# A recurrent mixer whose chunk steps are set further apart, with state sums of both tiles in one PSUM bank and outputs in the other

## The chip, the cores and the metric

The kernel runs on one core of one Trainium2 chip. The metric is the device time of one launch in microseconds (us). The program holds two whole transformer-like blocks; the change touches one part of the second, the recurrent mixer.

## The reference

The input is x of 256 tokens by 2048 channels. The first block is a state-space mixer beside a latent attention, followed by a convolutional feed-forward. The second block normalizes, projects once (`w_in`), runs two mixers on parts of the projection (a chunked state-space mixer and the recurrent one), multiplies both results by `w_out`, and ends in a gated feed-forward and a last norm. Of all this the recurrent mixer matters here:

```python
def step(S, inp):
    r_t, w_t, k_t, v_t, a_t, b_t = inp
    sa = jnp.einsum('bhvk,bhk->bhv', S, a_t)
    S = S * w_t[:, :, None, :] + sa[..., None] * b_t[:, :, None, :] + v_t[..., None] * k_t[:, :, None, :]
    return S, jnp.einsum('bhvk,bhk->bhv', S, r_t)
...
S0 = jnp.zeros((bsz, h, n, n), jnp.float32)
_, y = lax.scan(step, S0, seq)          # h = 32 heads, n = 64, 256 tokens
...
y = ((y - mu) * lax.rsqrt(var + GN_EPS)).reshape(b, s, D_RWKV) * gn_w + gn_b
y = y + bonus.reshape(b, s, D_RWKV)
return y * g
```

## The kernel before, in words

**Tiles, chunks and groups.** The 32 heads make 16 tiles (index j) of two heads, 128 partitions by 256 tokens. Two neighbouring tiles make a group (g = j // 2). The scan is done in 4 chunks (c) of 64 tokens: within a chunk the recurrence is a triangular system, which is inverted, and between chunks a 64x64 state per head is carried.

**TensorE's order is written out by hand.** `rwkv_phase` (L1618) runs three matrix products of 16 k-steps for each tile (keys, values, receptances: 48 k-steps a tile, 768 in all), then the first half of the output projection (16 products, 256 k-steps). After each k-step (three matmuls, L350 to L352) `gemm` calls `tick` (L311). All other work of TensorE comes from fibres: Python generators whose `yield n` means "go on after n more k-steps". So a `yield 4` puts the work of four k-steps, and whatever other fibres have in these four, between two pieces of a fibre. TensorE runs the result strictly in order: where the operand of a small product is late, all products behind it wait. `manual_schedule` does this for TensorE alone; the order on VectorE, ScalarE, GpSimd and SyncE (which issues the loads) is made by the framework's planner from its own estimates, each engine then running its list in order.

**The fibres.** For each tile `rwkv_k` (L1371) first multiplies the two low-rank factors `lw` by `twd` and `tad` into the bank `pn` (L1383, L1384), then sums squares per head (`head_scale`, L1347, into `pn` too); `rwkv_v` (L1416) transposes the values; `rwkv_r` (L1430) makes the matrices of a chunk (L1447), writes the upper blocks to DRAM (L1456), and for odd j starts `rwkv_group` just behind the first four of these matmuls. There is one `pn` bank, taken anew by each `ssq_start` (L413).

**The group.** `rwkv_group` (L1479) loads the blocks back in another layout (L1488), inverts 16x16 triangles with 30 small VectorE operations (L1495, L1497), writes them to DRAM (L1501) and reads them back (L1511). Then it yields `TK[6] + EX[g]` = 60 k-steps plus 0 to 18 (L1512). Behind that wait VectorE's transpose (L1519) and four rounds of small products into `pz` (L1528 to L1546), 7 k-steps apart, widen the inverse to 64x64 (`Lg`). Then come the chunks. Each has three steps:
- sums: `Km` x `Vc` plus `AR` x state into `WS`, for both tiles, and a copy of each to SBUF (L1572), then `yield TK[8][0]` = 4;
- solve: `Lg` times the copy, into `WS`, and two copies per tile of the halves into `UV` (L1580), then `yield TK[8][1]` = 4;
- outputs of both tiles (`outputs`, L1558), then the new state of both (L1587 to L1591), then `yield TK[8][2]` = 6.

A group is started every 96 k-steps. Two PSUM banks (`pcb`, L1324) are kept for the chunks: bank i holds the sums of tile i in its first 64 columns and the outputs of tile i in its upper half. Behind the last chunk the outputs go to SBUF (L1597), 14 k-steps later `head_scale` sums their squares in the `pn` bank (L1603), and 16 later the result is scaled, gated and stored.

**The low-rank weights** `lw` of tile j are loaded by SyncE at the head of tile j's loop (L1631) into one of six `ev` buffers, which the evacuations of products use as well.

Of the kernel before, what the change touches and what calls it, by code (L numbers as in the profile page):

```python
# [10 lines left out]
F32 = mybir.dt.float32  # L11
F32R = mybir.dt.float32r
I32 = mybir.dt.int32
AF = mybir.ActivationFunctionType
ALU = mybir.AluOpType
# [3 lines left out]
P = 128  # L19
T = 256  # L20
# [170 lines left out]
X0 = [(0, 2, 0, 4), (2, 2, 4, 4), (4, 4, 8, 8), (8, 4, 0, 0), (12, 4, 0, 0)]  # L191
PB = [0.0, 0.625, 1.0, 1.0, 0.625, 0.625]
EV = [(1, 2), (1, 4, 5, 8), 4, 1]
EX = [13, 14, 0, 0, 9, 9, 6, 18]
TK = [18, 17, (44, 19), (34, 12), 6, 10, 60, 7, (4, 4, 6), 14, 16]


class Sums:
# [26 lines left out]
class K:  # L225
# [1117 lines left out]
    @staticmethod  # L1343
    def c4(x):
        return x.rearrange("p (c t) -> p c t", c=4)
# [25 lines left out]
    def rwkv_k(self, st, pk):  # L1371
# [25 lines left out]
        G.tensor_scalar(PC, Pt[:, 63::64], 1.0, None, ALU.mult)  # L1397
        yield TK[0]
        p = self.ssq_start()
        spread = self.head_scale(p, [sq], "e", floor=1e-24)  # L1400
        yield TK[1]
        pn = spread(p[:, T:])
# [13 lines left out]
    def rwkv_v(self, st, pv):  # L1416
# [3 lines left out]
        self.shift_mix(pv, v, 32 + st["j"])  # L1420
        yield TK[2][st["j"] % 2]
        pt = self.ps(T).rearrange("p (c n) -> p c n", c=4)
# [7 lines left out]
    def rwkv_r(self, st, pr):  # L1430
# [9 lines left out]
        V.tensor_tensor(AR[:, :, 1], c4(r), c4(st["Pt"]), op=ALU.mult)  # L1440
        yield TK[3][j % 2]
        inc = self.incl.unsqueeze(1).to_broadcast([P, 4, 64])
        stt = self.strict.unsqueeze(1).to_broadcast([P, 4, 64])
        for z in (bz, kz):
# [19 lines left out]
            for h, hs in enumerate(halves):  # L1464
                V.tensor_tensor(Gs[halves[h ^ (z is kz)], h], pg[hs, :, 1], inc[hs], op=ALU.mult)
            yield TK[4]
        for z, sw in ((bz, 0), (kz, 1)):
# [3 lines left out]
            for h, hs in enumerate(halves):  # L1471
                S.activation(BK[halves[h ^ sw], h, 0:3], pt[hs, :, hs], AF.Copy)
            yield TK[5]
        pb = self.ps(T)
# [4 lines left out]
    def rwkv_group(self, g):  # L1479

        nc, A = self.nc, self.A
        V, G, S = nc.vector, nc.gpsimd, nc.scalar
# [8 lines left out]
        for s in range(15):  # L1491
            m, na = 15 - s, s // 2 + 1
            t = self.rw.tile([P, 64], F32, name=self.nm("ti"), tag="ti", bufs=1)
            t = t[:, :na * m].rearrange("p (i t) -> p i t", i=na)
# [7 lines left out]
        sl = slice(2 * (g % 2), 2 * (g % 2) + 2)  # L1502
        Lg, Ng = self.L[:, sl], self.Nc[:, sl]
# [3 lines left out]
        for h in range(2):  # L1507
            for sb, sr in enumerate((lo[h], hi[h])):
                for i in range(2):
                    o = 16 * i + 4 * (2 * h + sb)  # L1510
                    nc.sync.dma_start(Ld[sr, i], self.nd2[g][o:o + 4].rearrange("c s t -> s c t"))  # L1511
        yield TK[6] + EX[g]  # L1512

        def zt(i):
            return self.rw.tile([P, 2, 4, 32], F32, name=self.nm("zt"), tag=f"zt{i}", bufs=1)
# [8 lines left out]
        p = self.ps(tag="pz").rearrange("p (a i c t) -> p a i c t", a=2, i=2, c=4)  # L1524
# [14 lines left out]
        p = self.ps(tag="pz").rearrange("p (a i c t) -> p a i c t", a=2, i=2, c=4)  # L1539
# [9 lines left out]

        ts = [self.rs_.pop(2 * g + i) for i in range(2)]  # L1550
        halves = [slice(64 * h, 64 * h + 64) for h in range(2)]
        banks = self.pcb
        WS = [b[:, :64] for b in banks]

        def sv():
            return self.rw.tile([P, 64], F32, name=self.nm("sv"), tag="sv", bufs=10)

        def outputs(c, Sc):  # L1558
            for i, t in enumerate(ts):
                y = banks[i][:, T + 64 * c:T + 64 * c + 64]  # L1560
                self.pair2(y, lambda h: t["UV"][:, h, c], lambda h: t["Gs"][:, h, c], True, not c)
                if c:
                    self.pair(y, Sc[i], t["AR"][:, c, 1], False)

        Sc = [None, None]
        for c in range(4):
            ws, Ct = [sv(), sv()], [None, None]
            for i, t in enumerate(ts):
                self.pair(WS[i], t["Km"][:, c], t["Vc"][:, c], True, not c)
                if c:  # L1570
                    self.pair(WS[i], t["AR"][:, c, 0], Sc[i], False)
                V.tensor_copy(ws[i], WS[i])  # L1572
                if 0 < c < 3:
                    Ct[i] = sv()
                    S.activation(Ct[i], Sc[i], AF.Copy, scale=t["PC"][:, c:c + 1])
            yield TK[8][0]
            for i, t in enumerate(ts):
                self.pair(WS[i], Lg[:, i, c], ws[i])
                for h, hs in enumerate(halves):
                    V.tensor_copy(t["UV"][hs, h, c], WS[i][hs])  # L1580
            yield TK[8][1]
            outputs(c, Sc)
            if c < 3:
                Sn = [sv(), sv()]
                for i, t in enumerate(ts):
                    self.pair2(WS[i], lambda h: t["BK"][:, h, c], lambda h: t["UV"][:, h, c])
                    PC = t["PC"][:, c:c + 1]  # L1587
                    if c:
                        V.scalar_tensor_tensor(Sn[i], WS[i], PC, Ct[i], ALU.mult, ALU.add)
                    else:  # L1590
                        V.tensor_scalar(Sn[i], WS[i], PC, None, ALU.mult)  # L1591
            Sc = Sn
            if c < 3:
                yield TK[8][2]
        ys, sq = [self.rt("yc", bufs=4) for _ in range(2)], self.rt("sqc", 512, bufs=1)
        for i in range(2):
            S.activation(ys[i], banks[i][:, T:], AF.Copy)  # L1597
            S.activation(sq[:, T * i:T * i + T], ys[i], AF.Square)
        lw = self.rt("lw2", 512, 1)
        for i in range(2):  # L1600
            nc.sync.dma_start(lw[:, 256 * i:256 * i + 256], A["lora"][2 * g + i][:, 256:])
        yield TK[9]
        spread = self.head_scale(self.ssq_start(), [sq[:, :T], sq[:, T:]], "l")  # L1603
        yield TK[10]
        pn = spread(self.ps())
        pg = self.ps()
# [4 lines left out]
        for i, y in enumerate(ys):  # L1611
            j = 2 * g + i
# [5 lines left out]
    def rwkv_phase(self, xx):  # L1618
        nc, V = self.nc, self.nc.vector
        W = self.A["w_in2"]  # L1620
        self.rwkv_alloc()
        self.pl = 1
        self.rs_ = {}
        with self.tc.manual_schedule(engines={mybir.EngineType.PE}):
            for j in range(16):
                st = dict(j=j, bz=self.bz[:, j % 2], kz=self.kz[:, j % 2], AR=self.AR[j % 5])
                for x in ("Nc", "Gs", "UV", "BK"):
                    st[x] = getattr(self, x)[:, j % 4]
                self.rs_[j] = st
                st["lw"] = self.t(tag="ev")  # L1630
                nc.sync.dma_start(st["lw"], self.A["lora"][j][:, 0:256])  # L1631
                self.spawn(self.rwkv_k(st, self.gemm(W[60 + j], 16, xx)))
                self.spawn(self.rwkv_v(st, self.gemm(W[76 + j], 16, xx)))
                self.spawn(self.rwkv_r(st, self.gemm(W[44 + j], 16, xx)))

            xs = self.xx_new()
            for k in range(16):
                t = self.rows(self.ysd, k)
                self.split(xs(k), t, self.v("ssd_norm_g", k))
            for n in range(16):  # L1640
                h = self.t(tag="ev")
                nc.sync.dma_start(h, self.hd[:, n])
                V.scalar_tensor_tensor(h, h, self.v("final_norm_w", n), self.R1, ALU.mult, ALU.mult)
                V.tensor_tensor(h, h, self.gemm(self.A["w_out2"][n], 16, xs)[:, :T], op=ALU.add)
                nc.sync.dma_start(self.hd2[:, n], h)
            while self.fibs:
                self.tick()
# [173 lines left out]
```

## Time and profile before

| what | value |
|---|---|
| three runs | 3018.88 us median (3016.08 to 3033.33) |
| profiled execution | 3021.34 us, span 3019.6 us |
| mean granted TensorE clock over the span | 0.966 |
| TensorE busy (PE) | 2836.9 us, 94% |
| VectorE busy (DVE) | 1993.6 us, 66% |
| ScalarE busy (ACT) | 1521.0 us, 50% |
| GpSimd busy (POOL) | 1270.0 us, 42% |

Times in the rows are microseconds from the span's start unless marked ns. PE is TensorE's matmul stream, PEld its weight loads; SPq is SyncE's queue of DMA issues. PEclk is the granted clock as a share of full speed: 1.00 is 2.4 GHz, 0.50 is 1.2 GHz, and a mean between them says how much of a stretch was at either level. `out<-in` names tiles of the program; L350 is line 350 of the kernel before. `[0.99 <-DVE sv L1572]` behind a row is idle time of that engine just before it and what ended it. A row of a stretch reads: its start and end, its length, then for each engine in the order PE, PEld, DVE, ACT, POOL (only PE and PEld where the row is of one matmul line) the busy time and, in brackets, the count of instructions, then PEclk, the share of time that the DMA engines moved data, and GB/s.

### The profile page before, as it was taken

Reading aid. Unit: us, or ns where it says so; the run is one execution under the profiler, and the core shown is the slowest. Engines: PE = TensorE matmul, PEld = TensorE weight load, DVE = VectorE, ACT = ScalarE, POOL = GpSimd, SP = SyncE. Lnnn points to the kernel's source line nnn. Section 1 sums busy time; section 2 is a strip of 40 time slices with the busy share of each in tenths; the row PEclk is TensorE's granted clock in tenths of the full one; section 3 lists DMA queues with packets and bytes.
Section 4 is the critical chain, followed back from the end, with each engine's and each line's share of the span. In section 5 each row is a group of like instructions: output and inputs, shape, how many; then the busy total and the mean of one; then the engine's idle time right before and its main releaser. Section 6 shows DMA issues by size and latency. Waiting matters only on the chain.

```text
span 3019.6 us, 55057 instructions
## 1 busy us (share of the span) xinstructions
PE 2836.9 (94%) x21648; PEld 2550.1 (84%) x21648; DVE 1993.6 (66%) x3368; ACT 1521.0 (50%) x2553; POOL 1270.0 (42%) x877
## 2 busy tenths in 40 slices
PE   6766999999999999999989999989999999999998
PEld 6755988888888888999888888878888888888887
DVE  9994577885388866888676667775365554355544
ACT  6527655554455555555445444453354444444454
POOL 6555663333233334010365444445693333333333
PEclk8878999999999999999999999999999999999999
DMA  4222355556655566655443333345655556655564
GB/s 167 83 79 70 111 169 183 185 185 181 193 182 190 187 181 217 194 182 180 154 139 105 105 113 109 113 133 158 215 182 189 189 189 187 190 190 188 189 186 155
DMA packets 178981, 490.38 MB, mean 162 GB/s; under 512 B 44417, under 2 KB 61601, under 8 KB 178209
## 3 DMA queue, kind: packets, MB, share of 16 engines
q1 hardware_dynamic: 176992, 483.13, 50.9%
q8 instruction: 170, 2.79, 0.4%
q0 software_dynamic: 288, 2.10, 0.2%
q10 hardware_dynamic: 1440, 1.63, 0.2%
q14 instruction: 91, 0.74, 0.1%
HBM read 474.17 MB, written 12.62 MB: 161 GB/s over the span
## 4 chain that ended last, share of the span: by engine, by line
PE 70%; DVE 7%; DMA 3%; SPq 1%; issue 1%; ACT 1%; POOL 1%; DVEq 0%; POOLq 0%; ACTq 0%
PE acc L354 34%; PE acc L355 17%; PE acc L350 5%; PE acc L351 5%; PE acc L352 4%; DVE D L1497 1%; DVE ti L1495 1%; SPq L1511 1%; DMA i_d<-ev 1%; DMA ev<-h_d 1%; DVE X L1414 1%; POOL wl L336 1%; PE pc L1330 1%; PE py L1242 1%; ACT wh L330 0%
## 5 line engine op out<-in xcount | busy, mean ns | idle before, releaser
L330 ACT ACTIVATE wh<-raw 128x1024 fp32r<-128x1024 f32 (+2 forms) x873 | 908.0, 1041 | 998.5 <-PE acc L354 462.7
L336 POOL TENSOR_TENSOR wl<-raw,wh 128x1024 fp32r<-128x1024 f32 (+1 forms) x351 | 840.7, 2399 | 805.0 <-ACT wh L330 723.0
L336 DVE TENSOR_TENSOR wl<-raw,wh 128x1024 fp32r<-128x1024 f32 (+2 forms) x522 | 668.0, 1280 | 480.4 <-ACT wh L330 476.9
L354 PE MATMUL acc<-xx,wh 128*128 128x512 f32 x2496 | 886.3, 395 | 0.0
L355 PE MATMUL acc<-xx,wl 128*128 128x256 f32 x2496 | 704.2, 282 | 0.0
L350 PE MATMUL acc<-xx,wh 128*128 128x256 f32 x1968 | 599.2, 305 | 17.6 <-ACT wh L330 6.3
L352 PE MATMUL acc<-xx,wl 128*128 128x256 f32 x1968 | 568.8, 289 | 13.5 <-POOL wl L336 9.4
L351 PE MATMUL acc<-xx,wh 128*128 128x256 f32 x1968 | 569.0, 289 | 0.0
L354 PEld LDWEIGHTS acc<-xx,wh 128*128 128x128 f32 x2496 | 470.1, 188 | 110.8
L355 PEld LDWEIGHTS acc<-xx,wl 128*128 128x128 f32 x2496 | 469.0, 188 | 4.0 <-POOL wl L336 3.6
L350 PEld LDWEIGHTS acc<-xx,wh 128*128 128x128 f32 x1968 | 386.8, 197 | 30.8 <-ACT wh L330 6.9
L352 PEld LDWEIGHTS acc<-xx,wl 128*128 128x128 f32 x1968 | 387.0, 197 | 16.1 <-POOL wl L336 10.5
L351 PEld LDWEIGHTS acc<-xx,wh 128*128 128x128 f32 x1968 | 387.8, 197 | 2.5 <-issue 1.2
L354 PE MATMUL acc<-B,wh 128*128 128x512 f32 x960 | 341.1, 394 | 0.0
L355 PE MATMUL acc<-B,wl 128*128 128x256 f32 x960 | 269.6, 281 | 2.0 <-DVE wl L336 1.0
L354 PE MATMUL acc<-X,wh 128*128 128x512 f32 x640 | 230.6, 397 | 2.6 <-ACT wh L330 2.6
L391 POOL TENSOR_TENSOR ev<-ev,R 128x256 f32<-128x256 f32 x88 | 70.8, 804 | 353.5 <-PE acc L354 322.2
L354 PEld LDWEIGHTS acc<-B,wh 128*128 128x128 f32 x960 | 180.6, 188 | 41.7
L214 POOL TENSOR_TENSOR qa<-qa,sq 128x256 f32<-128x256 f32 x86 | 88.7, 1031 | 279.8 <-issue 132.2
L355 PE MATMUL acc<-X,wl 128*128 128x256 f32 x640 | 180.9, 283 | 1.9 <-POOL wl L336 1.9
L355 PEld LDWEIGHTS acc<-B,wl 128*128 128x128 f32 x960 | 179.8, 187 | 3.1 <-POOL wl L336 1.6
L354 PEld LDWEIGHTS acc<-X,wh 128*128 128x128 f32 x640 | 121.5, 190 | 29.9 <-ACT wh L330 2.8
(489 smaller groups left out, 4229.7 us busy)
## 6 DMA issues: line engine op xcount, KB each, us to landing
raw<-in_w_up_dram SPq DMA_DIRECT2D x264, 512.0 KB, 3.7
raw<-in_w_in_dram SPq DMA_DIRECT2D x213, 512.0 KB, 3.7
raw<-in_w_down_dram SPq DMA_DIRECT2D x128, 448.0 KB, 3.8
raw<-in_w_out_dram SPq DMA_DIRECT2D x96, 512.0 KB, 3.8
raw<-in_w_gate_dram SPq DMA_DIRECT2D x88, 512.0 KB, 4.2
raw<-in_w_down_dram SPq DMA_DIRECT2D x64, 512.0 KB, 4.1
raw<-in_w_glu_dram SPq DMA_DIRECT2D x8, 512.0 KB, 3.4
cb<-cs_d SPq DMA_DIRECT2D x16, 256.0 KB, 4.0
```

The source lines that it names most:

```text
L214: nc.gpsimd.tensor_tensor(self.acc, self.acc, sq, op=ALU.add)
L330: nc.scalar.activation(h, r, AF.Copy)
L336: eng.tensor_tensor(l, r, h.bitcast(F32), op=ALU.subtract)
L350: nc.tensor.matmul(p[:, :T], h, x[:, 1], start=first, stop=False)
L351: nc.tensor.matmul(p[:, :T], h, x[:, 0], start=False, stop=False)
L352: nc.tensor.matmul(p[:, :T], l, x[:, 0], start=False, stop=last)
L354: nc.tensor.matmul(p, h, x.rearrange("p a b -> p (a b)"), start=first, stop=False)
L355: nc.tensor.matmul(p[:, T:], l, x[:, 0], start=False, stop=last)
L391: (eng or nc.vector).tensor_tensor(out, s, mul, op=ALU.mult)
L1242: nc.tensor.matmul(yd[hs, P * b:P * b + P], xd[:, b, hs], d[:, h, b], start=True, stop=True)
L1330: self.nc.tensor.matmul(out[hs], lhsT[hs], rhs[hs], start=start, stop=stop)
L1414: V.tensor_tensor(st["kz"][hs, :, hs], c4(k)[hs], c4(Pi)[hs], op=ALU.mult)
```

## The change

The chunk steps are 7, 7 and 7 k-steps apart in place of 4, 4 and 6. The wait ahead of the inverse's first product is 56 k-steps for every group; the list `EX` is gone. The sums of both tiles stand side by side in the first of the two banks (`WS`, 128 columns) and the outputs of both in the second (`py`). One copy of 128 columns takes both sums to SBUF, and each half's copy into `UV` takes both tiles. The new states come ahead of the outputs. `head_scale` of the outputs sums in the outputs' bank and not in `pn`. The low-rank weights of tile j + 1 are loaded at the head of tile j, into a two-buffer tag (`th`) that nothing else uses in this phase.

```diff
--- before.py
+++ after.py
@@ -191,8 +191,7 @@
 X0 = [(0, 2, 0, 4), (2, 2, 4, 4), (4, 4, 8, 8), (8, 4, 0, 0), (12, 4, 0, 0)]
 PB = [0.0, 0.625, 1.0, 1.0, 0.625, 0.625]
 EV = [(1, 2), (1, 4, 5, 8), 4, 1]
-EX = [13, 14, 0, 0, 9, 9, 6, 18]
-TK = [18, 17, (44, 19), (34, 12), 6, 10, 60, 7, (4, 4, 6), 14, 16]
+TK = [18, 17, (44, 19), (34, 12), 6, 10, 56, 7, (7, 7, 7), 14, 16]
 
 
 class Sums:
@@ -1509,7 +1508,7 @@
                 for i in range(2):
                     o = 16 * i + 4 * (2 * h + sb)
                     nc.sync.dma_start(Ld[sr, i], self.nd2[g][o:o + 4].rearrange("c s t -> s c t"))
-        yield TK[6] + EX[g]
+        yield TK[6]
 
         def zt(i):
             return self.rw.tile([P, 2, 4, 32], F32, name=self.nm("zt"), tag=f"zt{i}", bufs=1)
@@ -1549,58 +1548,58 @@
 
         ts = [self.rs_.pop(2 * g + i) for i in range(2)]
         halves = [slice(64 * h, 64 * h + 64) for h in range(2)]
-        banks = self.pcb
-        WS = [b[:, :64] for b in banks]
-
-        def sv():
-            return self.rw.tile([P, 64], F32, name=self.nm("sv"), tag="sv", bufs=10)
-
-        def outputs(c, Sc):
-            for i, t in enumerate(ts):
-                y = banks[i][:, T + 64 * c:T + 64 * c + 64]
-                self.pair2(y, lambda h: t["UV"][:, h, c], lambda h: t["Gs"][:, h, c], True, not c)
-                if c:
-                    self.pair(y, Sc[i], t["AR"][:, c, 1], False)
+
+        WS = self.pcb[0][:, :P].rearrange("p (i n) -> p i n", i=2)
+        py = self.pcb[1].rearrange("p (i c n) -> p i c n", i=2, c=4)
+        UV = self.UV[:, sl]
+
+        def sv(w=64, tag="sv", bufs=6):
+            return self.rw.tile([P, w], F32, name=self.nm(tag), tag=tag, bufs=bufs)
 
         Sc = [None, None]
         for c in range(4):
-            ws, Ct = [sv(), sv()], [None, None]
+            ws, Ct = sv(P, "ws", 2).rearrange("p (i n) -> p i n", i=2), [None, None]
             for i, t in enumerate(ts):
-                self.pair(WS[i], t["Km"][:, c], t["Vc"][:, c], True, not c)
+                self.pair(WS[:, i], t["Km"][:, c], t["Vc"][:, c], True, not c)
                 if c:
-                    self.pair(WS[i], t["AR"][:, c, 0], Sc[i], False)
-                V.tensor_copy(ws[i], WS[i])
+                    self.pair(WS[:, i], t["AR"][:, c, 0], Sc[i], False)
                 if 0 < c < 3:
                     Ct[i] = sv()
                     S.activation(Ct[i], Sc[i], AF.Copy, scale=t["PC"][:, c:c + 1])
+            V.tensor_copy(ws, WS)
             yield TK[8][0]
-            for i, t in enumerate(ts):
-                self.pair(WS[i], Lg[:, i, c], ws[i])
-                for h, hs in enumerate(halves):
-                    V.tensor_copy(t["UV"][hs, h, c], WS[i][hs])
+            for i in range(2):
+                self.pair(WS[:, i], Lg[:, i, c], ws[:, i])
+            for h, hs in enumerate(halves):
+                V.tensor_copy(UV[hs, :, h, c], WS[hs])
             yield TK[8][1]
-            outputs(c, Sc)
             if c < 3:
+                for i, t in enumerate(ts):
+                    self.pair2(WS[:, i], lambda h: t["BK"][:, h, c], lambda h: t["UV"][:, h, c])
                 Sn = [sv(), sv()]
                 for i, t in enumerate(ts):
-                    self.pair2(WS[i], lambda h: t["BK"][:, h, c], lambda h: t["UV"][:, h, c])
                     PC = t["PC"][:, c:c + 1]
                     if c:
-                        V.scalar_tensor_tensor(Sn[i], WS[i], PC, Ct[i], ALU.mult, ALU.add)
+                        V.scalar_tensor_tensor(Sn[i], WS[:, i], PC, Ct[i], ALU.mult, ALU.add)
                     else:
-                        V.tensor_scalar(Sn[i], WS[i], PC, None, ALU.mult)
+                        V.tensor_scalar(Sn[i], WS[:, i], PC, None, ALU.mult)
+            for i, t in enumerate(ts):
+                self.pair2(py[:, i, c], lambda h: t["UV"][:, h, c], lambda h: t["Gs"][:, h, c], not i and not c, False)
+            if c:
+                for i, t in enumerate(ts):
+                    self.pair(py[:, i, c], Sc[i], t["AR"][:, c, 1], False, c == 3 and i == 1)
             Sc = Sn
             if c < 3:
                 yield TK[8][2]
         ys, sq = [self.rt("yc", bufs=4) for _ in range(2)], self.rt("sqc", 512, bufs=1)
         for i in range(2):
-            S.activation(ys[i], banks[i][:, T:], AF.Copy)
+            S.activation(ys[i], py[:, i], AF.Copy)
             S.activation(sq[:, T * i:T * i + T], ys[i], AF.Square)
         lw = self.rt("lw2", 512, 1)
         for i in range(2):
             nc.sync.dma_start(lw[:, 256 * i:256 * i + 256], A["lora"][2 * g + i][:, 256:])
         yield TK[9]
-        spread = self.head_scale(self.ssq_start(), [sq[:, :T], sq[:, T:]], "l")
+        spread = self.head_scale(self.pcb[1], [sq[:, :T], sq[:, T:]], "l")
         yield TK[10]
         pn = spread(self.ps())
         pg = self.ps()
@@ -1622,13 +1621,19 @@
         self.pl = 1
         self.rs_ = {}
         with self.tc.manual_schedule(engines={mybir.EngineType.PE}):
+            def lora(j):
+                t = self.t(tag="th")
+                nc.sync.dma_start(t, self.A["lora"][j][:, 0:256])
+                return t
+
+            lw = lora(0)
             for j in range(16):
-                st = dict(j=j, bz=self.bz[:, j % 2], kz=self.kz[:, j % 2], AR=self.AR[j % 5])
+                st = dict(j=j, lw=lw, bz=self.bz[:, j % 2], kz=self.kz[:, j % 2], AR=self.AR[j % 5])
                 for x in ("Nc", "Gs", "UV", "BK"):
                     st[x] = getattr(self, x)[:, j % 4]
                 self.rs_[j] = st
-                st["lw"] = self.t(tag="ev")
-                nc.sync.dma_start(st["lw"], self.A["lora"][j][:, 0:256])
+                if j < 15:
+                    lw = lora(j + 1)
                 self.spawn(self.rwkv_k(st, self.gemm(W[60 + j], 16, xx)))
                 self.spawn(self.rwkv_v(st, self.gemm(W[76 + j], 16, xx)))
                 self.spawn(self.rwkv_r(st, self.gemm(W[44 + j], 16, xx)))
```

## Rows read from the trace of the kernel before

**Rows 1.** Busy time by stretch: the 16 tiles' products, then the output projection.

```profile
1485.50:2025.30 539.80, 489.01 (x5641) 446.50 (x5640) 376.76 (x868) 255.37 (x508) 276.89 (x169) 0.95 0.38 114
2025.30:2167.50 142.20, 133.22 (x1434) 124.01 (x1432) 74.28 (x180) 54.69 (x94) 78.54 (x34) 0.94 0.56 177
```

**Rows 2.** What TensorE waited for, 1480 to 2200: total us, times, longest.

```profile
PE pc L1330 <- DVE sv L1572: 21.2, 18, 4.1
PE pc L1335 <- DVE B L1580: 11.7, 8, 1.8
PE pn L1383 <- DVE hnl L1359: 6.6, 2, 3.3
PE pn L1383 <- DMA ev<-in_lora_dram: 4.8, 1, 4.8
```

**Rows 3.** TensorE in order of time, two k-steps and a solve (L1330) that waits.

```profile
1753.89 0.28 PE L350 MATMUL acc<-xx,wh 128*128 128x256 f32 x1
...
1754.25 0.28 PE L350 MATMUL acc<-xx,wh 128*128 128x256 f32 x1
...
1755.75 0.47 PE L1330 MATMUL pc<-sv,hh 64*64 64x64 f32 x8 [0.99 <-DVE sv L1572]
```

**Rows 4.** VectorE in order of time beside Rows 3.

```profile
1752.13 2.94 DVE L1414 TENSOR_TENSOR X<-kvr,rv 64x256 f32<-64x256 f32 x2
...
1755.48 0.35 DVE L1572 COPY sv<-pc 128x64 f32<-128x64 f32 x2
```

**Rows 5.** The k-steps by the count of one of their three matmuls (L351), by stretch.

```profile
1485.50:2025.30 539.80, 221.49 (x767) 152.46 (x768) 0.95 0.38 114
...
1546.60:1581.00 34.40, 16.01 (x56) 11.04 (x56) 0.95 0.35 104
1604.60:1651.10 46.50, 16.59 (x56) 11.80 (x56) 0.89 0.33 98
...
2043.90:2081.70 37.80, 16.81 (x57) 11.91 (x57) 0.90 0.40 114
```

**Rows 6.** Instructions on the chunks' banks: ns min/median/max of each.

```profile
L1580 DVE COPY B<-pc x128: 205/222/229, 1609.8 to 2129.4; 64x64 f32<-64x64 f32 x128
L1572 DVE COPY sv<-pc x64: 177/218/226, 1608.4 to 2126.8; 128x64 f32<-128x64 f32 x64
```

**Rows 7.** The same for line 382, a PSUM read of 256 columns.

```profile
L382 DVE TENSOR_TENSOR ev<-acc,R x92: 359/424/426, 399.1 to 2028.2; 128x256 f32<-128x256 f32 x92
```

**Rows 8.** TensorE: a wait on `pn`, and a k-step matmul behind it.

```profile
1866.24 0.70 PE L1383 MATMUL pn<-twd,ev 128*128 128x256 f32 x2 [3.30 <-DVE hnl L1359]
...
1867.85 0.42 PE L351 MATMUL acc<-xx,wh 128*128 128x256 f32 x1
```

**Rows 9.** TensorE: group 0 starts (L1447), and a load comes late.

```profile
1546.63 1.13 PE L1447 MATMUL pm<-hh,X 128*128 128x128 f32 x8 [1.41 <-DVE X L1411]
...
1577.06 0.94 PE L1383 MATMUL pn<-twd,ev 128*128 128x256 f32 x2 [4.77 <-DMA ev<-in_lora_dram]
```

**Rows 10.** SyncE's issues in the same stretch, and VectorE's transpose behind them.

```profile
1572.84 1.82 SPq L1501 DMA_DIRECT2D m_d<-D  x4
1574.76 0.39 SPq L1631 DMA_DIRECT2D ev<-in_lora_dram  x1
...
1575.97 3.65 SPq L1511 DMA_DIRECT2D Ld<-m_d  x8
...
1583.95 0.44 DVE L1519 STREAM_TRANSPOSE zt<-Ld 128x256 f32<-128x256 f32 x1
```

**Rows 11.** Group 1: start, transpose. Group 7: start, transpose.

```profile
1604.61 1.13 PE L1447 MATMUL pm<-hh,X 128*128 128x128 f32 x8 [0.84 <-DVE X L1411]
1640.76 0.43 DVE L1519 STREAM_TRANSPOSE zt<-Ld 128x256 f32<-128x256 f32 x1
2043.92 0.55 PE L1447 MATMUL pm<-hh,X 128*128 128x128 f32 x1 [0.65 <-DVE X L1411]
2080.36 0.45 DVE L1519 STREAM_TRANSPOSE zt<-Ld 128x256 f32<-128x256 f32 x1 [6.76 <-DMA Ld<-m_d]
```

## The prediction

> **What bounds the kernel now.** I read the page first: TensorE is busy 94% of the span and no other engine over 66%, so a change in the mixer pays only through TensorE's own queue there. Then the busy times of the two stretches in which the mixer's fibres run [rows 1]: 489.0 of 539.8 us, then 133.2 of 142.2. TensorE stands idle for 50.8 + 9.0 = 59.8 us, and VectorE, busy 377 of 540 us, is the next engine but 163 us from full. Third, TensorE's waits by releaser over the same stretch [rows 2]: 21.2 us for the copies of the sums, 11.7 us for the copies of the halves, 6.6 us for a small VectorE read of the `pn` bank, 4.8 us for one load of low-rank weights: 44.3 us. Fourth, the granted clock [rows 1]: 0.95 and 0.94. At half speed work takes twice as long, so the loss is at most 0.05 x 539.8 + 0.06 x 142.2 = 27.0 + 8.5 = 35.5 us. A fall follows a wait: behind an idle of 3.30 us a k-step matmul takes 0.42 us [rows 8], against 0.28 at full clock [rows 3].
>
> Why the copies are late is seen where VectorE's list is laid beside one such wait. Two operations of another fibre, 64x256, take 2.94 us, and the copies run only behind them, at 1755.48 [rows 4]; TensorE gets its operand at 1755.75 after 0.99 us of idling [rows 3]. So it is VectorE's order and not the copy's length (0.22 us [rows 6]) that makes the wait, and distance in k-steps is what covers it. A bare k-step is 0.36 us [rows 3]; with all fibres between, the mean is 539.8 / 768 = 0.70 us [rows 1, 5].
>
> **Steps further apart.** 4 becomes 7 ahead of the solve and ahead of the outputs, 6 becomes 7 ahead of the next sums. Three more k-steps give 3 x 0.36 = 1.1 us at least and 3 x 0.70 = 2.1 us on average. The 26 waits of the two kinds hold 32.9 us, 1.27 us each, the longest 4.1 and 1.8 [rows 2]. With 1.1 us off each, the first kind keeps about 21.2 - 17 x 1.1 = 2.5 us at the mean; but they are unequal (one of 4.1 keeps 3.0), so I keep 8 us there and 1 us of the second kind. That is a gain of 24 us; the ends are 0 (the copies are put off in VectorE's list by as much as TensorE goes on) and 32.9. The chain becomes longer, 3 x 21 + 14 = 77 k-steps against 50, but the next group's comes 96 later, so it delays nobody; nothing is late behind it but the outputs of the last group, which have more than 50 k-steps to spare in the output projection.
>
> **One copy for two tiles.** A read of 64 columns takes 0.22 us, one of 256 columns 0.42 [rows 6, 7]: from this I estimate 0.29 us for 128 columns. Per step two copies become one (0.44 to 0.29), four become two (0.89 to 0.58). Over 32 steps this takes 32 x 0.46 = 15 us of VectorE's time, off the path and so nothing by itself; the outputs' operand is ready 0.3 us earlier, the solve's of the first tile about 0.3 us later (it now waits for the second tile's sums). I set both to 0, with 32 x 0.3 = 10 us as the bound on either side. New states ahead of the outputs: the same matmuls in another order, so 0 for TensorE; the cover for the next sums grows by the outputs' length.
>
> **The outputs' sum of squares leaves `pn`.** The two waits of 3.3 us [rows 2, 8] are low-rank products that need the `pn` bank while VectorE has not yet read these sums. In the outputs' bank they meet nobody: that bank is written next by the following group, some 20 k-steps later. Gain 6.6 us; with the ends 0 (the read still queues, for another user) and 6.6.
>
> **The low-rank weights a tile earlier.** The one late load was issued at 1574.76, right behind issues that had stood on VectorE's solve until 1572.84 [rows 10]; TensorE got it at 1577.06 [rows 9]. Issued 48 k-steps earlier it passes that solve's issues and some six weight loads. Those weights move behind one small load (0.39 us of SyncE's time), which their four buffers cover. The `th` buffer it needs was last read 32 k-steps before. Gain 4.8 us. For tiles 0 and 1 the buffers come from the mixer before, and SyncE may stand for them: not shown, between 0 and the 4.8 of the late load; I take 0, since TensorE has 16 k-steps of weights buffered there.
>
> **56 k-steps ahead of the inverse.** This is the new wait. From a group's first matrix product to the inverse's operand runs a chain over DRAM that the k-steps don't shorten. In group 0 the product starts at 1546.63 [rows 9], the last issue of the read back ends at 1579.62, and VectorE's transpose ends at 1584.39 [rows 10]: 37.8 us. The 56th k-step stands at 1581.0 [rows 5], and without the late load at 1581.0 - 4.8 = 1576.2. So TensorE, which went on to 73 k-steps there, would now stand up to 8.2 us, or less where the transpose is put right behind the load. I take 6. In group 7 the transpose waits for the load and ends at 2080.81 [rows 11]; the 56th k-step is at 2081.7 [rows 5], and with 3 us of waits and slow clock gone there, at 2078.7: 2 us. In group 1 the chain takes 1641.19 - 1604.61 = 36.6 us [rows 11] against 46.5 [rows 5]; groups 2 to 6 are as group 1. Even with 6 us of chunk waits out of it, that is 40: 0. Cost 8 us, with the ends 2 and 20 (2.5 a group). Behind this wait stand the k-steps of the running product; every engine fed by TensorE waits with them.
>
> **The clock.** Where waits go, falls go. Of the 35.5 us some stays: the border to the output projection, where 4.1 us of idle and a heavy VectorE remain, about 7, and group 0's new wait, about 3. Of the other 25 I take two thirds: 16 us. Ends 0 and 25.
>
> **The sum:** -24 - 6.6 - 4.8 + 8 - 16 = -43 us against the profiled execution of 3021.3 us, so 2978; the median of the runs is 2.5 us lower. I forecast 2977 us, -1.4%. A difference under 1% (30 us) is one that a measurement of this kernel can hardly tell from none.
>
> **The rivals.**
> - *All of it goes.* Only 4 us of the chunk waits stay, the new wait is 2 and the clock gives 25: 3021 - 29 - 11.4 + 2 - 25 = 2958. For it: the mean slack gained, 2.1 us, is above the mean wait. Against: VectorE's operations of 2.9 us fall at other places now. Chance 0.12.
> - *The waits come back elsewhere.* VectorE, at 70% and in order, is late for other operands once TensorE is faster; a third of the 24 us holds, the clock gives 5, the new wait costs 8: 3021 - 8 - 11.4 - 5 + 8 = 3005. For it: long VectorE operations stand in every 96 k-steps, and each step meets them at one place or another. Against: 7 k-steps are 2.5 us bare, close to the 2.94 of [rows 4]. Chance 0.25.
> - *The inverse's chain becomes the bound, and it is slower.* The place is L1528 in every group. It decides as soon as 56 k-steps take less than the chain's 37 us, which needs either the chain 5 us longer (its solve behind more VectorE work, its issues behind more weight loads) or k-steps at 0.6 us. At 10 us longer: groups 1 to 6 some 7 us each, group 0 16 and group 7 12, in all 70; the clock then gives nothing: 3021 - 24 - 11.4 + 70 = 3056. For it: two groups are already over the edge. Against: in groups 1 to 6 the stretch has 10 us of room before the gains. Chance 0.05.
> - *Sharing a bank costs.* The sums of both tiles lie in one bank, so that TensorE's write of the second tile and VectorE's read of the first can't overlap as they do in two banks; with one copy for both, each solve waits 0.3 us more, and where it is late anyway that is 32 x 0.3 = 10 us: 2987. Against: the copy comes behind other VectorE work in most steps, as in [rows 4]. Chance 0.08. The Trainium skill, page "PSUM — Partial Sum Buffer", section "PSUM bank collisions raise a hardware error", says that two engines must not touch the same bank and partition quadrant at once and that the chip does not arbitrate, so the order must be kept by semaphores per bank. By that rule the outputs, now in the other bank, are freed of the state's reads, and the sums are tied together; no row here shows two engines on one bank at once.
>
> The forecast's own case has 0.50 and the range 2962 to 2995.
>
> **How the numbers follow.** Likeliest time 2977. The range takes in the case of all gains and that of waits coming back: 2953 to 3010. Faster by over 1%, that is under 2989: 0.45 of the forecast's 0.50, 0.11 of the first rival and half of the last, 0.04: 0.60. Within 1%: 0.05 + 0.25 + 0.04 + 0.01 = 0.35. Slower by over 1%: 0.05.
>
> **What the changed kernel's profile would show.** Right: waits of L1330 and L1335's successors on the copies down from 32.9 us to under 10; no wait of the low-rank products; a wait of some 6 us for the inverse's first product in group 0 and little in the others; granted clock 0.97 or more; the first stretch of [rows 1] some 30 to 40 us shorter. Wrong: that first product waits in most groups, or the waits on copies hold over 20 us, or the clock stays at 0.95 though the waits are gone.

## The result: 1% slower, where 1.4% faster was forecast

The changed kernel takes 3058.8 us at the median of its runs (3044.9 to 3060.8) against 3018.9 before: the ratio, taken of the means, is 1.0106, 95% interval [1.0071, 1.0141]. The profiled execution took 3044.9 us and is the fastest of its runs, so its trace shows only a part of the loss: 23.5 us of span.

Its busy times by stretch, cut where the k-steps of the tiles and of the output projection begin and end, as in [rows 1]:

```profile
1490.20:2042.80 552.60, 480.19 (x5680) 440.77 (x5679) 384.34 (x792) 256.96 (x511) 275.54 (x169) 0.94 0.36 111
2042.80:2192.20 149.40, 131.47 (x1395) 123.11 (x1395) 74.39 (x162) 54.38 (x94) 78.88 (x34) 0.94 0.55 172
```

The two stretches grew by 12.8 and 7.2 us; the phase also began 5 us later, which is not the change's (nothing ahead of it differs). TensorE's idle time went from 59.8 us to 72.4 + 17.9 = 90.3, and the granted clock went from 0.95 and 0.94 to 0.94 and 0.94. Lines are those of the kernel that a row is from; in the changed kernel most stand one lower than before (L1114 is now L1113). What TensorE waited for, 1480 to 2220 (total us, times, longest), against [rows 2]:

```profile
PE pc L1329 <- DVE ws L1569: 36.0, 12, 5.0
PE pm L1446 <- DVE yc L1614: 12.9, 5, 2.6
PE pz L1527 <- DVE zt L1518: 8.3, 1, 8.3
PE pc L1334 <- DVE B L1574: 7.5, 3, 3.9
PE pm L1469 <- DVE yc L1612: 5.1, 1, 5.1
```

The waits on `pn` and on the late load, 11.4 us in [rows 2], are gone; a low-rank product waits 1.7 us once for another VectorE read of `pn`. The waits on the copies, which were to fall from 32.9 us to 9, rose to 43.5. Two waits are new: 18 us for the scaling of the outputs at a group's end, and 8.3 us for group 0's inverse.

Why does a copy come late that has 7 k-steps now? One more piece of work matters here. Each block of weights, 128x1024, is split in two: ScalarE's copy is the high part (`wh`), and the block less this copy is the low part (`wl`), which the third matmul of a k-step takes. In this phase GpSimd does that subtraction. VectorE in order of time ahead of one (L1569), then the wait of TensorE behind it, then GpSimd's list in the same stretch:

```profile
1788.33 2.38 DVE L1113 SCALAR_TENSOR_TENSOR kvr<-ev,vec,kvr 128x255 f32<-128x255 f32 x1 [2.05 <-ACT kvr L1112]
1790.74 2.50 DVE L1439 TENSOR_TENSOR hh<-kvr,rv 128x256 f32<-128x256 f32 x1
1793.16 0.47 DVE L1403 SCALAR_TENSOR_TENSOR rv<-kvr,vec,pn 128x256 f32<-128x256 f32 x1
...
1795.71 0.29 DVE L1569 COPY ws<-pc 128x128 f32<-128x128 f32 x1
```

```profile
1796.06 0.69 PE L1329 MATMUL pc<-ws,hh 64*64 64x64 f32 x8 [3.53 <-DVE ws L1569]
```

```profile
1788.03 4.93 POOL L335 TENSOR_TENSOR wl<-raw,wh 128x1024 fp32r<-128x1024 f32 x2 [1.63 <-ACT wh L329]
```

Two GpSimd subtractions run from 1788.03 to 1792.96, and each of the two VectorE operations of 255 and 256 columns beside them lasts 2.4 to 2.5 us and ends shortly behind one of them. The same lines take 0.41 to 0.48 us where they are short. Over the whole phase (ns min/median/max), first L1113 of the changed kernel, then the same line with GpSimd's subtractions moved to VectorE (run `f2_after_dve`):

```profile
L1113 DVE SCALAR_TENSOR_TENSOR kvr<-ev,vec,kvr x48: 459/2294/2387, 1512.2 to 2056.5; 128x255 f32<-128x255 f32 x48
```

```profile
L1113 DVE SCALAR_TENSOR_TENSOR kvr<-ev,vec,kvr x48: 473/478/485, 1511.4 to 1968.7; 128x255 f32<-128x255 f32 x48
```

So in the changed kernel 32 of these 48 operations, those over 0.7 us, are held up by GpSimd. Over the whole phase, from the first low-rank product to the last store of the projection, 83 VectorE operations of the changed kernel last over 0.3 us more than the shortest of their line and shape, 156 us more in all; in the kernel before there are 76, with 138 us. Each of them overlaps a GpSimd subtraction. In the runs `f1_before_dve` and `f2_after_dve`, where GpSimd makes none, one such operation is left.

The pair of operations that the prediction took for a long VectorE run, 2.94 us [rows 4], is of the same kind: in the kernel before, one of GpSimd's subtractions stands beside it:

```profile
1752.21 2.57 POOL L336 TENSOR_TENSOR wl<-raw,wh 128x1024 fp32r<-128x1024 f32 x1 [3.64 <-ACT wh L330]
```

The Trainium skill says so on the page "SBUF — State Buffer", section "SBUF: two separate sides": a VectorE operation with two SBUF inputs and a GpSimd operation that reads SBUF need the same port pair; whoever starts first holds it for the whole instruction, and the other is blocked. The rows agree; the copies, which read PSUM, are not lengthened themselves (0.29 us above, at most 0.23 us for all of [rows 6]) but stand in line behind what is.

The new wait for the scaling has the same cause. VectorE, TensorE behind it, and GpSimd:

```profile
1683.19 2.47 DVE L1457 SCALAR_TENSOR_TENSOR kvr<-kvr,vec,kvr 128x256 f32<-128x256 f32 x1
1685.59 0.41 DVE L1614 TENSOR_TENSOR yc<-yc,pm 128x256 f32<-128x256 f32 x1
```

```profile
1686.05 2.08 PE L1446 MATMUL pm<-hh,X 128*128 128x128 f32 x8 [2.63 <-DVE yc L1614]
```

```profile
1682.83 2.55 POOL L335 TENSOR_TENSOR wl<-raw,wh 128x1024 fp32r<-128x1024 f32 x1 [5.46 <-ACT wh L329]
```

The program hands out two `pm` banks in turn, and the end of a group takes both, one for the spread sums (read by L1612) and one for the gate (read by L1614). The product L1446 takes a `pm` bank next and has to wait until L1614 has read it; in front of L1614 stands L1457, held from 0.48 to 2.47 us by a subtraction. This is so in all five waits of this kind; ahead of the sixth, 5.1 us for the bank that L1612 reads, L1648 is held twice (2.60 and 2.23 us).

### The profile page after: what moved, and what is told of

Same layout as the page of the kernel before. It is cut to its first block, busy times and chain, and to the rows that moved or that the text cites. A ratio compares the mean times of both kernels' runs of the same rounds, so it can differ in the third digit from the quotient of the medians.

```text
span 3043.1 us, 54949 instructions
## 1 busy us (share of the span) xinstructions
PE 2826.2 (93%) x21648; PEld 2543.3 (84%) x21648; DVE 2004.5 (66%) x3272; ACT 1521.5 (50%) x2553; POOL 1267.5 (42%) x877
## 4 chain that ended last, share of the span: by engine, by line
PE 69%; DVE 8%; DMA 3%; issue 1%; POOL 1%; ACT 1%; SPq 1%; POOLq 0%; DVEq 0%; ACTq 0%
PE acc L353 34%; PE acc L354 17%; PE acc L349 5%; PE acc L350 4%; PE acc L351 4%; DVE ti L1494 1%; DVE D L1496 1%; POOL wl L335 1%; DVE kvr L1113 1%; ACT wh L329 1%; PE pm L1446 1%; DMA N<-n_d 1%; PE pc L1329 1%; DMA raw<-in_w_in_dram 0%; DVE kvr L1457 0%
## 5 line engine op out<-in xcount | busy, mean ns | idle before, releaser
L351 PE MATMUL acc<-xx,wl 128*128 128x256 f32 x1968 | 567.8, 289 | 15.1 <-POOL wl L335 11.0
L351 PEld LDWEIGHTS acc<-xx,wl 128*128 128x128 f32 x1968 | 385.8, 196 | 18.2 <-POOL wl L335 12.5
```

The source lines that it names most:

```text
L351: nc.tensor.matmul(p[:, :T], l, x[:, 0], start=False, stop=last)
```

## The experiments

Theories. **1**: the place of a step beside VectorE's long runs decides. **2**: the shared bank and joint copies make the copies late. **3**: the 56 k-steps do. **4**, formed after the first four runs: GpSimd's subtractions lengthen VectorE's operations, and that makes most waits, in the kernel before too. Each ratio below is to the kernel before on the same chip, with its 95% interval; a gap between kernels that were measured beside different runs of the kernel before is taken from their ratios.

**`a1_form_only`**: the old `TK` and `EX` in the changed kernel.

> Everything of the change but the distances: steps 4, 4, 6 apart and 60 k-steps plus the per-group extra ahead of the inverse, as before. Theory 1 (where a step falls beside the long VectorE runs of the keys fibre and of the solve decides, not how far apart the steps are): the waits of before on the copies stay, 33 us, and the 11 us on the pn bank and the late load go: 3005 to 3015 us, at or below the kernel before. Theory 2 (one bank and one copy for both tiles make the copies late): over 3035. Theory 3 (56 k-steps for every group are what costs): as theory 1.

3011.5 us, ratio 0.9961 [0.9945, 0.9978]. The new form gains 12 us of 3024, about the 11.4 that its two waits hold in [rows 2]. Theory 2 falls: with the same bank and joint copies, the waits on the copies are 25.6 and 13.0 us, 38.6 in all against 32.9, and the kernel is faster all the same.

**`a2_dist_only`**: `TK` of the changed kernel in the old form, with `head_scale(banks[1][:, P:T], ...)`.

> The distances alone (7, 7, 7 and 56) on the old form: two banks with sums and outputs of one tile each, a copy for each tile, outputs ahead of the states, low-rank weights loaded late. The sum of squares goes to the second chunk bank, since it can't share pn at this distance. Theory 1: as slow as the changed kernel, 3050 to 3070, with waits of some 36 us on the sums' copies and 13 us for the last scaling at the same places. Theory 2: the added distance helps where the form is old, 2980 to 3010. Theory 3: 3030 to 3040.

3030.6 us, 1.0020 [1.0003, 1.0037]: neither theory's number. The waits on the scaling are there (12.8 and 5.0 us), but those on the sums' copies are 9.5 us, not 36, with 12.1 us for the states. VectorE's list around the chunks has nearly the same order in both kernels; which of its operations last 2.5 us differs. That is where theory 4 came from. The late load is back here (4.7 us) and the inverse of group 0 waits 3.3 us; with the load early it waits 8.3 in the changed kernel: the load's gain was only handed on to that wait.

**`a3_end_later`**: `TK[10]` 16 to 28.

> The changed kernel with the group's last step 28 and not 16 k-steps behind the sum of squares, so that its six VectorE operations come behind the first matrix product of the odd tile and not ahead of it. Theory 1: the 12.9 us of that product's wait on them and most of the 5.1 us of the other go, 10 to 18 us off the changed kernel's 3059. Theories 2 and 3: no change beyond 5 us.

3021.5 us, 0.9996 [0.9977, 1.0016], 1.1% or 33 us off the changed kernel, twice the expected: the 18 us of waits on the scaling are gone, and the sums' copies cost 15.6 us in place of 36.0. L1457 keeps its 0.48 us here. Part comes back elsewhere: the halves' copies rise from 7.5 to 17.5 us, and L1446 waits 10.3 us for an operand.

**`a4_666`**: `(7, 7, 7)` to `(6, 6, 6)`.

> The changed kernel with steps 6, 6, 6 apart. The sums of the last chunk then come 9 k-steps earlier in the 96, ahead of the keys fibre's VectorE run of the even tile and not behind it. Theory 1: the waits of the last chunk on its sums' copy, 3.4 to 5.0 us in each group, go for the most part, though the next copies (the halves) may then meet that run: 10 to 25 us faster than the changed kernel's 3059. Theories 2 and 3: less distance, so each late step waits one k-step (0.36 us) more: the same or up to 10 us slower.

3009.8 us, 0.9951 [0.9935, 0.9968]: 47 us off the changed kernel by less distance. Its two largest waits:

```profile
PE pc L1329 <- DVE ws L1569: 18.4, 6, 3.4
PE pz L1527 <- DVE zt L1518: 8.2, 1, 8.2
```

The forecast's rule, more k-steps, fewer waits, is wrong in sign here.

**`b1_666_end4`**: steps 6, 6, 6 and `TK[10]` 27, so that the end falls where the changed kernel has it.

> Steps 6, 6, 6 as in the run at 3010 us, but the group's last step put back to where the changed kernel has it, one k-step behind the odd tile's keys fibre (27 in place of 16 k-steps behind the sum of squares). Theory 1 (places decide): the 13 us of wait of the next matrix product on the last scaling come back and with them what they push back: 3025 to 3045. If the last step's place alone explains the changed kernel, 3040 or more; if the last chunk's place alone, 3005 to 3015 as without the move.

3015.8 us, 0.9976 [0.9959, 0.9993]: 0.25% or 8 us of loss from that place, against 33 us in `a3_end_later`. The waits for the scaling are 5.4 and 2.6 us here, in place of 12.9 and 5.1. The place of the end is not worth a fixed price either.

**`b2_57`**: `TK[6]` 56 to 57.

> The changed kernel with 57 k-steps in place of 56 ahead of the inverse, all else the same, so every chunk step falls one k-step later. Theory 1: every step still stands behind the same VectorE run, so the same within 8 us of 3059. Theory 4 (the 28 us between the changed kernel and the old form at the same distances are chance: where GpSimd's 2.4 us operations fall on VectorE's): at least 12 us faster.

3034.3 us, 1.0047 [1.0029, 1.0066]: one k-step takes 0.6% or 18 us off (25 by the medians). Places alone, which hardly changed, don't do that; the sums' copies still cost 33.7 us.

**`c1_after_no_low`, `c2_before_no_low`**: `piece` returns the high part twice and skips the subtraction where `pl` is 1 and a k-step has three matmuls. These two kernels leave out the low parts, so they do not compute the reference; TensorE's matmuls stay the same in number.

```diff
+        if self.pl == 1 and self.one:
+            return h, h
```

> The changed kernel without GpSimd's work in this phase: the low parts of the weights are not made in the recurrent mixer and the first output projection, and TensorE multiplies the high parts in their place, the same matmuls. So no GpSimd operation of 2.4 us runs beside VectorE. Theory 4: VectorE's operations keep their short form (0.2 to 0.5 us), the waits on the copies fall from 36 us to under 10, and the kernel comes under 2990. Theory 1 with places alone: long runs stay, waits of 20 us or more, over 3020.

> The kernel before without GpSimd's low parts in the same way. Theory 4: its waits on the copies fall as well, from 33 us to 10 to 15, and with VectorE on time the changed kernel without them is faster than this one by what was forecast from distance, the pn bank and the load (10 to 30 us). Theory 1 with places alone: this one is the faster, as with the low parts.

2896.0 us, 0.9589 [0.9565, 0.9613], and 2902.5 us, 0.9600 [0.9584, 0.9616]. The condition also holds in parts of the first block, so 43 to 46 us of both lie ahead of the phase; from the first low-rank product to the last store of the projection the changed kernel goes from 687 to 587 us, the one before from 668 to 592. The largest waits, of the changed kernel and then of the one before:

```profile
PE pm L1610 <- ACT B L1429: 4.2, 6, 2.8
PE pz L1529 <- DVE zt L1520: 3.2, 2, 2.8
```

```profile
PE acc L356 <- ACT wh L330: 4.6, 4, 1.3
PE acc L357 <- POOL wl L338: 2.8, 2, 1.9
```

Without GpSimd's subtractions beside VectorE the waits on the copies hold 0.7 us or less in all in either kernel, at 4 k-steps or at 7: theory 4 in its plainest form. The changed kernel was expected to be 10 to 30 us the faster here; it is 6.5, and the intervals overlap. The distances had been given to a wait that is not made by distance.

**`d1_after_split4`, `d2_before_split4`, `d3_666_split4`**: nothing is left out, but each subtraction of GpSimd is done in four pieces of 256 columns.

```diff
-        eng.tensor_tensor(l, r, h.bitcast(F32), op=ALU.subtract)
+        w = 2 * P if self.one and eng is nc.gpsimd else nb * P
+        for o in range(0, nb * P, w):
+            q = slice(o, o + w)
+            eng.tensor_tensor(l[:, q], r[:, q], h.bitcast(F32)[:, q], op=ALU.subtract)
```

> The changed kernel with each of GpSimd's 1024-column subtractions in this phase done as four of 256 columns. Theory 4 (a VectorE operation that meets one of them lasts until it is over, 2.3 us in place of 0.2 to 0.5): the longest such operation falls to about 1 us, the waits on the copies from 36 to under 15 us, 3000 to 3025. Theory 1 (places alone): no gain, since GpSimd's time only grows (some 0.75 us each, 3.0 in place of 2.4): 3055 to 3070.

> The kernel before with the same split. Theory 4: its 33 us of waits fall as well, 2985 to 3010, and the gap to the changed kernel with the split shrinks to under 15 us. Theory 1: 3015 to 3030, the gap stays at 30 us or more.

> Steps 6, 6, 6 with the split. Theory 4: 2980 to 3000, the best of the three. Theory 1: no better than without the split, 3005 to 3020.

2985.6 us (0.9861 [0.9828, 0.9894]), 2978.1 (0.9838 [0.9805, 0.9870]) and 2965.0 (0.9804 [0.9768, 0.9839]): 74, 48 and 45 us gained, and the gap of the changed kernel to the one before shrinks to 7.5 us. All three are faster than expected. Some 14 to 23 us of each lie ahead of the phase, where the split acts as well. GpSimd works more for it (from 1485 to 2100 us, 106 subtractions of 2.40 us, 254 us busy, become 465 of 0.79 us, 351 us busy, as neighbours overlap in the record), and L1113 of the changed kernel, three lines lower here, now has:

```profile
L1116 DVE SCALAR_TENSOR_TENSOR kvr<-ev,vec,kvr x48: 471/711/1115, 1490.7 to 1994.5; 128x255 f32<-128x255 f32 x48
```

An operation of this line that meets GpSimd now lasts 1.12 us at the most, no more than a piece and its own time together. The waits on the sums' copies fell less than expected, from 36.0 to 24.9 us.

**`d4_666_dve`, `f1_before_dve`, `f2_after_dve`, `f3_666_dve_g0`, `f4_form_dve`**: `self.pl = 1` becomes 0 in `rwkv_phase`, so that VectorE makes all low parts there; `d4` and `f3` with steps 6, 6, 6, `f3` with 13 more k-steps for group 0, `f4` with the distances of before.

> Steps 6, 6, 6, with the low parts of the weights in this phase made by VectorE (1.28 us for 1024 columns) and none by GpSimd. Theory 4: the lengthened operations go (some 95 us of VectorE's time), 128 x 1.28 = 164 us come in, VectorE gets to about 85% and its list longer: 2990 to 3020, with waits of short operations only. Theory 1: VectorE's runs get longer, 3030 or more.

> The kernel before with all low parts of this phase made by VectorE. Theory 4 (GpSimd's operations lengthen VectorE's and so make most waits): 2960 to 2985, waits on the copies under 20 us, the waits of the low-rank products on pn and on the late load still there.

> The changed kernel with the same. Theory 4 together with the forecast's terms for distance, pn and load: 5 to 25 us faster than the kernel before with the same. If the change is worth nothing in itself: within 5 us of it. If steps 7, 7, 7 are misplaced whatever the length of VectorE's operations (theory 1): slower than it by 10 us or more.

> The fastest so far (2959 us, steps 6, 6, 6, low parts by VectorE) with 69 in place of 56 k-steps ahead of the inverse in group 0 alone. Its wait of 8.3 us goes: 2948 to 2956. If the wait only covers other lateness: no change.

> The new form at the old distances (4, 4, 6 and 60 plus the extra), low parts by VectorE. If the distances are what pays: slower than steps 7, 7, 7 with the same by 5 us or more. If the form alone does (pn, load): the same as those.

| low parts by VectorE | us | ratio |
|---|---|---|
| before (`f1`) | 2956.0 | 0.9760 [0.9725, 0.9795] |
| changed (`f2`) | 2961.7 | 0.9777 [0.9737, 0.9818] |
| steps 6, 6, 6 (`d4`) | 2959.4 | 0.9774 [0.9746, 0.9802] |
| the same, group 0 later (`f3`) | 2954.8 | 0.9754 [0.9719, 0.9788] |
| new form, old distances (`f4`) | 2948.3 | 0.9737 [0.9702, 0.9771] |

`d4` was measured beside other runs of the kernel before than the rest. VectorE gets some 126 operations of 1.23 us more, and still the waits on the copies end: 1.6 us in `f2`, 3.2 in `f1`, 3.6 in `f4`. The operations that were held are at their short times throughout, as the row of `f2` above shows for L1113. `d4` and `f1` are faster than expected; in `d4` VectorE, expected to be 85% busy, is busy 392 of 530 us (1490 to 2020). What is left of waits in `f2` and then in `f4`:

```profile
PE pz L1527 <- DVE zt L1518: 10.2, 5, 8.0
PE pz L1540 <- DVE zt L1518: 4.6, 1, 4.6
PE pm L1608 <- ACT B L1427: 3.8, 6, 2.4
```

```profile
PE pm L1447 <- DVE X L1411: 4.4, 1, 4.4
PE pn L360 <- ACT sq L210: 3.0, 1, 3.0
PE pz L1541 <- DVE zt L1519: 2.8, 1, 2.8
PE pz L1528 <- DVE zt L1519: 2.1, 1, 2.1
```

The expectation of `f2` failed: at 7, 7, 7 and 56 it is not faster than the kernel before with the same, but about 6 us slower (the intervals overlap). Against `f4`, the same form at the old distances, it loses 13 us; by the waits 10 of them are at the inverse's early products (14.8 us against 4.9). `f3` is not told apart from `d4`: the inverse's waits fall from 11.6 to 7.0 us, but the intervals overlap. The waits of the low-rank products, which `f1` was expected to keep, are nearly gone there. None is left on the load, and of the 6.6 us on `pn` this:

```profile
PE pn L1383 <- DVE hnl L1359: 1.3, 2, 0.8
```

`f4` beats both kernels: 76 us, or 2.6%, under the one before.

## Why the prediction was wrong, step by step

- **Steps further apart, -24 us: this step failed.** It said that "it is VectorE's order and not the copy's length (0.22 us [rows 6]) that makes the wait, and distance in k-steps is what covers it", and carried the waits of before over, less 1.1 us each. But the 2.94 us of [rows 4] were two operations of 0.42 us of work (the median of that line, x32), one of them held up by GpSimd; GpSimd's operations follow the weights of the same k-steps, and moving the steps moves what they meet. Measured: 43.5 us of waits on the copies in place of 32.9. Where nothing is held, the old 4 k-steps leave 3.2 us of them (`f1`) or 0.7 (`c2`), so distance has next to nothing to cover. The rival that had them come back elsewhere was right in kind, and much too small at 3005 us.
- **The end of a group at no cost: failed.** The sum said that the longer chain "delays nobody": it looked at who needs the outputs, not at the `pm` banks that their scaling holds. The scaling now falls just ahead of a later tile's products, which take these banks, with held VectorE operations in front of it: 12.9 + 5.1 us of waits, and 33 us by `a3_end_later`, which changes other waits too. The place alone does not cost this: in `f2`, with the end at the same place, no such wait is left.
- **pn, -6.6, and the load, -4.8.** Right in amount: both waits are gone and the form alone gains 12 us (`a1_form_only`). But they too came for the most part from held operations: with the low parts on VectorE the old form keeps 1.3 us of the one and nothing of the other (`f1`). In the changed kernel the load's part is lost again, as 56 k-steps make group 0 wait for its inverse.
- **56 k-steps, +8.** Right: 8.3 us in group 0, no such wait in others with GpSimd as it was. Group 7's 2 us did not come. With VectorE on time, the phase is shorter and other groups wait as well (`f2`, 5 times).
- **One copy for two tiles, 0.** Right within what the runs can tell: `a1_form_only` has no loss, and a copy of 128 columns takes 0.28 to 0.29 us, as estimated. The rival of the shared bank is not borne out.
- **The clock, -16.** It hung on the waits; they stayed, and so did the clock at 0.94. With most of the waits gone it rose: 0.98 from 1490 to 2100 us in `f4` and in `d4`, against 0.94 in the changed kernel.
- **The forecast.** Its own sum less 2.5 us gives 2975.5 and not 2977; this changes nothing.

Still open: why the changed kernel loses 26 us on the old form at the same distances. One k-step of shift (`b2_57`) takes off nearly as much, which speaks for chance in which operations meet GpSimd's, with the pattern then repeated in each group; no run shows it for that pair. The amount of held time does not decide it: 156 us in the changed kernel, 139 in the old form at its distances, but 158 in `b2_57`, which is faster. It is more likely what stands behind a held operation that counts, which is not shown.

## What to carry to other kernels

Before distance is put between an operation and its user, compare the operation's neighbours in the queue with their own shortest time: a minimum of 0.46 us beside a median of 2.29 on one line was the sign here that another engine held it, and that engine's list beside it was the proof. Then the cure is to shorten or move that engine's operations, here for 48 us in the kernel before (14 of them ahead of the phase), and 68 where VectorE took the work. In an order written by hand, a step's cover depends on what it meets and not on a count alone; moving all steps at once changes all that they meet, so move one and measure. A wait taken away ahead of a chain with a fixed length (here the round trip over DRAM) is only handed on to the next one.

## What the runs showed of the hardware that was not expected

A VectorE operation with both inputs in SBUF that meets one of GpSimd's subtractions ends only shortly behind it: up to 2.7 us beside 128x1024 in 2.40, at most 1.1 us beside 128x256 in 0.79, in place of 0.17 to 0.48 alone. One operation with a single SBUF input was held as well: L1387 of the kernel before, an addition and a multiplication by constants on 128x256, takes 0.25 us at its shortest and 2.46 beside a subtraction. Operations that read PSUM, as the copies [rows 6] and L382 [rows 7], and the transposes (L1519, 0.43 to 0.45 us) were not. VectorE makes the low part of 1024 columns in 1.23 us where GpSimd takes 2.40, so taking the work away from the engine that had time for it made the phase of the kernel before shorter, from 668 us to 601.
